# The last layer of a two-block model carries 512 token columns instead of 528

## The chip, the cores and the metric

The kernel runs on one NeuronCore of a Trainium2 chip. The core has a matrix engine (TensorE, in the profile PE, with the loading of its weights as PEld), a vector engine (VectorE, DVE), a scalar engine (ScalarE, ACT), GpSimd (POOL) and SyncE (SP), which issues most DMA transfers. Each engine works off its own list of instructions in order; semaphores join the lists. The metric is the device time of one execution, in microseconds (us), as the median of the runs.

## The reference

Two blocks of two layers each, in float32, on 512 tokens of 1024 features. The first block isn't touched here. The second puts 16 learned meta tokens ahead of the 512 real ones (528 in all) and runs `hybrid_layer` twice; only the real tokens are returned:

```python
h = jnp.concatenate([meta, x], axis=1)              # 16 + 512 tokens
for i in range(DEPTH):                              # DEPTH = 2
    h = hybrid_layer(h, ...)
return rmsnorm_2(h, final_norm)[:, N_META:]

def hybrid_layer(h, ...):
    proj = rmsnorm_2(h, attn_norm_g) @ w_in          # fq fk fv flog rq rk rv rg
    fox = fox_attention(fq, fk, fv, logf)            # 8 heads of 64, causal, with forget gates
    ret = retention_chunkwise(rotate(rq), rotate(rk), rv)      # 4 heads of 128
    mix = concat(fox, silu(rg) * head_groupnorm(ret))
    h = h + mix @ w_out
    hn = rmsnorm_2(h, ffn_norm_g)
    return h + (silu(hn @ w_gate) * (hn @ w_up)) @ w_down      # 2816 hidden features
```

Attention and retention are causal, so the real tokens need the meta tokens' keys and values. Of the second layer nothing else of the meta tokens reaches the output.

## The kernel before, in words

Activations lie feature-major: 128 features on the partitions, the 528 tokens as columns, eight such tiles for 1024 features. Every large product is done in `gemm` (lines 188 to 197). A float32 operand is split into a high part of 11 mantissa bits and a rest; three products (lines 195, 196, 197) stand for one. So an output tile of 128 features takes 8 k-tiles x 3 products per group of columns. A product writes at most 512 columns (one PSUM bank), and `groups` (line 199) cuts 528 into two groups of 264: a tile is 48 products of 264 columns. In block 1, which has 512 tokens, a tile is 24 products of 512.

`wunit` (line 163) brings 512 KB of weights: a DMA issued by SP, the high part on ACT (line 170), the rest on DVE (line 171); three buffers for each.

`layer2` (line 1720) does in this order, for each of the two layers:
- it writes the eight tiles of the residual to DRAM (`xs`), makes the forget gates, and the attention's values by token (`values2`, lines 1532 to 1534, products of 512 columns, and 1529 and 1530 for the meta tokens);
- four pairs of attention heads (loop at 1752): the query tile and the key tile of the pair (`proj2`, DVE at 1765 applies the norm), then `fox_pair`: first the meta tokens' own queries (`fox_meta`, lines 1550 to 1577), then four blocks of 128 queries, each with scores (1593, 1599), mask, maximum, exponential, division, transposes (1618, 1628) and the weighted values (1633, 1637);
- `values2` for the retention, then four heads (loop at 1780): query and key tile with rotation (`rotated`, DVE at 1651 to 1654), then `retention` (scores 1667 and 1674, values 1683 to 1688, group norm with transposes at 1710);
- four gate tiles (loop at 1790), the output projection (8 tiles) added to the reloaded residual, a norm (`lead`, `lead_end`, `spread`), 22 pairs of gate and up tiles (`up`, 1826), and the down projection in six pieces (1852; k of 2, 4, 4, 4, 4, 4 tiles), added to the residual by DVE at 211.

PSUM has eight banks: four slots S of one bank and two slots D of two banks. In the attention and in the heads of the retention the large products have two S slots and the small ones the other two; elsewhere the large products have all four. A tile of 264 columns takes a whole slot as well.

A scheduling layer sets the order on each engine. It takes instructions by priority, and within a layer by their place in the code, as their inputs come ready by its own estimates, and so puts the next pair's or head's large products between the small ones of the attention. What it has set is fixed in the program.

Of the kernel before, what the change touches and what calls it, by code (L numbers as in the profile page):

```python
# [113 lines left out]
class Kern:  # L114
# [10 lines left out]
    # ------------------------------------------------------------------ tiles  # L125
# [19 lines left out]
    def band(self, b):  # L145
        """Instructions inside take the scheduling priority b (less is sooner)."""
# [7 lines left out]
    def many(self, ring, cnt, rows, n, dt=F32):  # L154
        """cnt aps [rows, n] and their tiles; short ones share a tile by twos."""
# [6 lines left out]
    # ---------------------------------------------------------------- weights  # L162
# [20 lines left out]
    def split(self, src, hi, lo):  # L183
        """hi: 11 mantissa bits of src, lo: the other 12."""
# [3 lines left out]
    def gemm(self, o, ts, w, k_w, x):  # L188
        """o += w[:, k_w[i]].T @ x[i][:, ts] over i, in three passes."""
# [14 lines left out]
    def acc_tile(self, pg, wu, ks, h, x, n, ga):  # L204
        """x += ga * (w @ h)"""
# [20 lines left out]
    def sq_add(self, ring, accs, x, i, n, cnt=KT):  # L226
        """Sum of squares of cnt tiles in two tiles: all but the last, the last."""
# [51 lines left out]
    def norm_split(self, ring, rb, out, xs, n, A, sh, ks=range(KT)):  # L279
        """h = x * rstd * A (+ sh), as hi / lo parts."""  # L280
# [15 lines left out]
    # ----------------------------------- norm whose scale is applied afterwards  # L296
    def lead(self, ring, k, x, g, hl, acc, first=None):
        """Residual tile k [128, 528] is final: x * g as hi / lo parts, sum of squares.

        first = (gain, its square, sum of squares before the gain): x is scaled by the gain in place first.  # L300
        """
        nc = self.nc
        xl = x[:, NM:L2]
# [22 lines left out]
        elif k == KT - 1:  # L326
            sq = ring.new([P, L2])
            nc.scalar.activation(sq, x, AF.Square)
            self.rest = (sq[:, NM:L2], self.ones[:, 0:1], sq[:, 0:NM], sq)
        else:  # L330
            sq = ring.new([P, L2])
# [12 lines left out]
    def lead_end(self, ring, pr, acc, acc1=None):  # L344
        """1/rms by token rows: columns 0-3 for the real tokens, column 4 for the meta tokens."""
# [1374 lines left out]
    def layer2(self, l):  # L1720
# [8 lines left out]
        for k in range(KT):  # L1729
            nc.sync.dma_start(out=xs[k], in_=X[k])  # L1730
# [368 lines left out]
```

## Time and profile before

| what | us |
|---|---|
| median of three runs (3163.07 to 3173.02) | 3165.82 |
| profiled execution: its span (no other time of it is given) | 3163.6 |
| PE busy in the span | 3064.9 |
| DVE busy | 1892.6 |
| ACT busy | 1182.7 |
| last layer from its first attention pair to the end | 2480.7 to 3163.6 |
| of this, the MLP behind the output projection, to the end of its last product | 2757.1 to 3147.2 |

A matmul's duration in the profile runs from its entry to the modelled end of its pipeline, so successive ones overlap; 264 columns take 285 ns, but the next begins 122 ns later. What a stream of them costs is read from how many begin in a stretch, or from the start of one to the start of the next. Start times are us from the span's start.

### The profile page before, as it was taken

The page shows a single profiled execution, that of the slowest core. Times are in us where ns is not written, and L with a number is a line of the kernel's source. Part 1 is how long each engine was busy: PE and PEld are TensorE (multiplying, and loading weights), DVE is VectorE, ACT ScalarE, POOL GpSimd, SP SyncE. Part 2 cuts the span into 40 slices and gives each one's busy share as a digit, 9 for nine tenths or more (in the row PEclk, how much of TensorE's full clock was granted, in tenths as well). Part 3 has the DMA queues.
Part 4 walks back from the last instruction along what each step waited for, and adds up shares of the span by engine and source line. Part 5 has one row for each costly group of instructions (what it writes and reads, how often), then busy time and mean ns, then how long its engine had stood idle before and what let it go on. Part 6 is the DMA issues. An engine that isn't in the chain of part 4 may idle for free.

```text
span 3163.6 us, 48896 instructions
## 1 busy us (share of the span) xinstructions
PE 3064.9 (97%) x19434; PEld 2687.5 (85%) x19434; DVE 1892.6 (60%) x3935; ACT 1182.7 (37%) x2119; POOL 105.4 (3%) x287
## 2 busy tenths in 40 slices
PE   8899899999999998999999999999999999999998
PEld 4778879788888877778888888999999888999998
DVE  5877756787655766444436656555555556555554
ACT  4545554253333455433334431322223331322222
POOL 1000000000000000000000000000001000000000
PEclk9999999999999999999999999999999999999999
DMA  8554526755555432122333212232323212322222
GB/s 302 171 193 144 159 91 191 234 164 171 172 166 170 131 118 60 61 80 93 94 99 110 66 54 71 95 91 90 92 89 110 65 54 71 95 90 92 92 89 67
DMA packets 138147, 367.55 MB, mean 116 GB/s; under 512 B 14864, under 2 KB 42960, under 8 KB 137920
## 3 DMA queue, kind: packets, MB, share of 16 engines
q1 hardware_dynamic: 135760, 361.72, 36.2%
q8 instruction: 153, 2.51, 0.3%
q10 hardware_dynamic: 1728, 2.24, 0.2%
q14 instruction: 74, 0.61, 0.1%
q0 software_dynamic: 432, 0.48, 0.1%
HBM read 349.16 MB, written 15.12 MB: 115 GB/s over the span
## 4 chain that ended last, share of the span: by engine, by line
PE 83%; DVE 6%; DMA 6%; ACT 3%; issue 1%; POOL 1%; SPq 0%; ACTq 0%; DVEq 0%; POOLq 0%
PE S L195 21%; PE S L196 21%; PE S L197 21%; DVE wl L171 2%; PE S L1006 1%; DMA wr<-wmod 1%; PE D L978 1%; ACT wh L170 1%; PE S L1637 1%; PE D L1593 1%; PE S L994 1%; PE S L1532 1%; DVE wr L428 1%; PE S L1534 1%; PE D L1688 1%
## 5 line engine op out<-in xcount | busy, mean ns | idle before, releaser
L195 PE MATMUL S<-A,wh 128*128 128x264 f32 (+2 forms) x5104 | 1619.3, 318 | 14.6 <-ACT A L290 3.8
L197 PE MATMUL S<-A,wl 128*128 128x264 f32 (+2 forms) x5104 | 1613.5, 316 | 7.1 <-DVE wl L171 7.0
L196 PE MATMUL S<-A,wh 128*128 128x264 f32 (+2 forms) x5104 | 1611.6, 316 | 3.8 <-DVE A L291 2.4
L195 PEld LDWEIGHTS S<-A,wh 128*128 128x128 f32 x5104 | 965.1, 189 | 87.2 <-issue 8.0
L197 PEld LDWEIGHTS S<-A,wl 128*128 128x128 f32 x5104 | 964.8, 189 | 71.4 <-DVE wl L171 11.1
L196 PEld LDWEIGHTS S<-A,wh 128*128 128x128 f32 x5104 | 964.5, 189 | 70.0 <-DVE A L291 5.7
L170 ACT CAST wh<-wr 128x1024 fp32r<-128x1024 f32 (+1 forms) x474 | 495.1, 1045 | 1393.1 <-PE S L196 838.6
L171 DVE TENSOR_TENSOR wl<-wr,wh 128x1024 fp32r<-128x1024 f32 (+1 forms) x474 | 576.3, 1216 | 346.5 <-ACT wh L170 336.0
L428 DVE SCALAR_TENSOR_TENSOR wr<-wr,B 128x512 f32<-128x512 f32 x224 | 149.2, 685 | 84.1 <-DMA wr<-wmod 84.0
L213 DVE SCALAR_TENSOR_TENSOR A<-S,mod,A 128x512 f32<-128x512 f32 x144 | 107.7, 749 | 114.4 <-PE S L197 114.1
L211 DVE TENSOR_TENSOR A<-A,S 128x264 f32<-128x264 f32 x224 | 93.7, 426 | 116.5 <-PE S L197 116.3
L186 DVE TENSOR_TENSOR A<-A,A 128x512 fp32r<-128x512 f32 (+3 forms) x168 | 102.3, 618 | 32.8 <-ACT A L185 32.5
L1834 DVE TENSOR_TENSOR A<-S,A 128x264 f32<-128x264 f32 x88 | 38.0, 432 | 121.1 <-PE S L197 115.5
L185 ACT CAST A<-A 128x512 fp32r<-128x512 f32 (+3 forms) x168 | 93.1, 562 | 24.8 <-DVE A L1799 18.1
L1842 DVE SCALAR_TENSOR_TENSOR A<-A,S 128x264 f32<-128x264 f32 x88 | 37.8, 429 | 80.4 <-PE S L197 75.8
L1006 PEld LDWEIGHTS S<-B,B 128*128 128x128 f32 x416 | 53.6, 195 | 17.1 <-issue 5.5
L1006 PE MATMUL S<-B,B 128*128 128x96 f32 x416 | 55.7, 277 | 4.7 <-ACT A L1011 2.3
L223 POOL TENSOR_TENSOR rnr<-rnv,mhalf 128x4 f32<-128x4 f32 (+1 forms) x19 | 23.2, 1223 | 969.3 <-DVE rnv L222 581.5
L978 PE MATMUL D<-A,A 96*128 96x256 f32 (+1 forms) x144 | 54.6, 483 | 0.5 <-ACT A L948 0.5
L562 DVE SCALAR_TENSOR_TENSOR A<-A,cw,A 128x512 f32<-128x512 f32 (+1 forms) x84 | 52.8, 638 | 2.4 <-ACT A L559 0.8
L1061 ACT ACTIVATE A<-A 128x512 f32<-128x512 f32 x80 | 50.6, 632 | 2.2
L230 ACT ACTIVATE A<-A 128x512 f32<-128x512 f32 (+1 forms) x66 | 33.6, 535 | 46.9 <-DVE A L213 35.1
(402 smaller groups left out, 2903.2 us busy)
## 6 DMA issues: line engine op xcount, KB each, us to landing
wr<-wmod SPq DMA_DIRECT2D x112, 512.0 KB, 4.1
wr<-wup SPq DMA_DIRECT2D x96, 512.0 KB, 3.6
wr<-wdn SPq DMA_DIRECT2D x96, 512.0 KB, 3.8
wr<-win SPq DMA_DIRECT2D x78, 512.0 KB, 4.0
wr<-wg SPq DMA_DIRECT2D x44, 512.0 KB, 3.5
wr<-wu SPq DMA_DIRECT2D x44, 512.0 KB, 3.6
wr<-wd SPq DMA_DIRECT2D x44, 512.0 KB, 3.5
wr<-wout SPq DMA_DIRECT2D x40, 512.0 KB, 3.7
```

Source lines behind the costliest of these rows:

```text
L170: nc.scalar.copy(hi, raw)
L171: nc.vector.tensor_sub(lo, raw, hi.bitcast(F32))
L185: self.nc.scalar.copy(hi, src)
L186: self.nc.vector.tensor_sub(lo, src, hi.bitcast(F32))
L195: nc.tensor.matmul(o, wh[:, k_w[i]], xh[:, ts], start=(i == 0), stop=False)
L196: nc.tensor.matmul(o, wh[:, k_w[i]], xl[:, ts], start=False, stop=False)
L197: nc.tensor.matmul(o, wl[:, k_w[i]], xh[:, ts], start=False, stop=(i == nk - 1))
L211: nc.vector.tensor_add(x[:, ts], x[:, ts], ps)
L213: nc.vector.scalar_tensor_tensor(out=x[:, ts], in0=ps, scalar=ga, in1=x[:, ts], op0=ALU.mult, op1=ALU.add)
L428: nc.vector.scalar_tensor_tensor(out=wf if i == len(which) - 1 else self.junk, in0=wf, scalar=1.0, in1=self.cb[s * 2 + hf], op0=ALU.mult, ...
L978: nc.tensor.matmul(sc[:, off : off + nk], qT[h][:, ts], kT[h], start=True, stop=True)
L1006: nc.tensor.matmul(yp, pT[:, kt], V[j][:, h * MD : h * MD + MD], start=(kt == 0), stop=(kt == tot // P - 1))
```

## The change

In the last layer the queries, the gates, the retention's outputs and all behind them (out projection, norm, MLP, final norm) are made for the 512 real tokens alone, in one group of 512 columns. Keys, values, forget gates and the rotation's tables keep 528. `fox_meta` and the retention's meta outputs go, as do the meta column of the two norms behind. Layer 0 is as it was.

```diff
 def layer2(self, l):
+    final = l == DEPTH - 1
+    n = N if final else L2
+    o0 = L2 - n
+    every = self.groups(L2)
+    kept = [slice(o0, L2)] if final else every
-    xs = self.tl(self.dr, [KT, P, L2], F32, f"xt{l}")
+    xs = self.tl(self.dr, [KT, P, n], F32, f"xt{l}")
...
-            for o, ts in self.proj2(pg, l, which * 4 + p2, h):
+            for o, ts in self.proj2(pg, l, which * 4 + p2, h, every if which else kept):
...
-        self.fox_pair(pm, p2, two[0], two[1], v, vblk, mix[p2])
+        self.fox_pair(pm, p2, two[0], two[1], v, vblk, mix[p2], not final)
...
-        q = self.rotated(qr, pg, l, 8 + hd, h, rope)
+        q = self.rotated(qr, pg, l, 8 + hd, h, rope, kept)
...
-        k = self.rotated(qr, pg, l, 12 + hd, h, rope)
-        o = A.new([P, L2])
-        before = self.retention(pm, l, hd, q, k, v, o)
+        k = self.rotated(qr, pg, l, 12 + hd, h, rope, every)
+        o = A.new([P, n])
+        before = self.retention(pm, l, hd, q, k, v, o, kept)
...
-        for o, ts in self.proj2(pg, l, 16 + hd, h):
+        for o, ts in self.proj2(pg, l, 16 + hd, h, kept):
...
-    X = [A.new([P, L2]) for _ in range(KT)]
+    X = [A.new([P, n]) for _ in range(KT)]
...
-        for ts in self.groups(L2):
+        for ts in self.groups(n):
...
-                self.acc_tile(pg, w, kk, hs, X[m], L2, None)
+                self.acc_tile(pg, w, kk, hs, X[m], n, None)
 def proj2(self, pg, l, m, h, tss):
-    for ts in self.groups(L2):
+    for ts in tss:
 def fox_pair(self, pr, p2, q, k, v, vblk, o, meta):
-    self.fox_meta(pr, q, k, vb, o)
+    if meta:
+        self.fox_meta(pr, q, k, vb, o)
 def retention(self, pr, l, hd, q, k, v, out, tss):
-    for ts in self.groups(L2):
+    for ts in tss:                                   # scores with the meta keys
...
-    nc.tensor.matmul(om, pmt[:, 0:NM], v[4][:, hs], start=True, stop=True)
+    if meta:
+        nc.tensor.matmul(om, pmt[:, 0:NM], v[4][:, hs], start=True, stop=True)
...
-    for rows, cnt, src in ((NM, 1, om.unsqueeze(1)), (P, 4, ot)):
+    for rows, cnt, src in ([(NM, 1, om.unsqueeze(1))] if meta else []) + [(P, 4, ot)]:
 def lead_end(self, ring, pr, acc, acc1=None):
-    tok.append((4, NM, acc[:, 0:NM], sm_, one))
+    if meta:
+        tok.append((4, NM, acc[:, 0:NM], sm_, one))
 def spread(self, rb, r, meta):
+    if rb.shape[-1] == N:
+        for t in range(4):
+            o = dd[:, 0, t * P : t * P + P]
+            nc.tensor.matmul(o, r[:, t : t + 1].broadcast_to([P, P]), self.ident, start=True, stop=True)
+        nc.scalar.copy(rb, dd[:, 0])
+        return
```

The order on the engines moves where the attention and the retention of the last layer stand. Line numbers of the changed kernel are its own. On PE, in the first attention pair, third block of queries (S and D are PSUM slots, B the probabilities, wh and wl a weight unit's parts), before:

```order
L1618 MATMUL S_4229_23080<-ident_69,B_4228_23075 128x128 x3
L1599 MATMUL D_4247_23139<-A_4180_22894,A_4173_22830 128x264 x2
L197 MATMUL S_4268_23249<-A_4064_22243,wl_4267_23245 128x264
L195 MATMUL S_4268_23249<-A_4066_22245,wh_4266_23244 128x264
L196 MATMUL S_4268_23249<-A_4067_22246,wh_4266_23244 128x264
L197 MATMUL S_4268_23249<-A_4066_22245,wl_4267_23245 128x264
L1618 MATMUL S_4235_23098<-ident_69,B_4234_23093 128x128 x3
L1628 MATMUL S_4237_23104<-ident_69,metaP_4224_23067 32x128
L195 MATMUL S_4268_23249<-A_4068_22247,wh_4266_23244 128x264
L196 MATMUL S_4268_23249<-A_4069_22248,wh_4266_23244 128x264
L197 MATMUL S_4268_23249<-A_4068_22247,wl_4267_23245 128x264
L195 MATMUL S_4268_23249<-A_4070_22249,wh_4266_23244 128x264
```

and in the changed kernel, where transposes are line 1637, scores 1618 and weighted values 1652 and 1656:

```order
L1637 MATMUL S_4222_23033<-ident_69,B_4221_23028 128x128 x3
L1618 MATMUL D_4234_23072<-A_4178_22866,A_4172_22829 128x264
L1637 MATMUL S_4228_23051<-ident_69,B_4227_23046 128x128 x3
L1618 MATMUL D_4240_23092<-A_4179_22867,A_4173_22830 128x264
L1647 MATMUL S_4230_23057<-ident_69,metaP_4217_23020 32x128
L1618 MATMUL D_4240_23092<-A_4179_22867,A_4173_22830 128x264
L1652 MATMUL S_4232_23061<-mT_4231_23059,A_4155_22809 128x128
L1656 MATMUL S_4232_23061<-B_4223_23037,A_4150_22797 64x128
...
L1656 MATMUL S_4232_23061<-B_4229_23055,A_4150_22797 64x128
...
L195 MATMUL S_4254_23138<-A_4078_22257,wh_4252_23133 128x512
```

Before, large products of 264 columns stood between the transposes and the weighted values of this block; now none does until the block is done, and the ones that follow have 512 columns.

On DVE, in the fourth block of the same pair, before (1765 reads the next pair's query and key tiles out of PSUM, 264 columns at a time, between the softmax's steps):

```order
L1608 TENSOR_SCALAR mx_4242_23123<-mx_4242_23123 128x1
L1604 TENSOR_TENSOR D_4247_23139<-D_4247_23139,fmask_14888 128x128
L1765 TENSOR_TENSOR A_4257_23176<-S_4262_23212,A_4121_22566 64x264
L1607 TENSOR_REDUCE mx_4248_23143<-D_4247_23139 128x1
L1613 RECIPROCAL smx_4243_23124<-smx_4243_23124 128x1
L171 TENSOR_TENSOR wl_4351_23591<-wr_4349_23589,wh_4350_23590 128x1024
L1614 TENSOR_SCALAR B_4244_23127<-B_4244_23127,smx_4243_23124 128x528
L186 TENSOR_TENSOR A_4157_22814<-S_4239_23108,A_4156_22813 128x128
L1608 TENSOR_SCALAR mx_4248_23143<-mx_4248_23143 128x1
L1622 COPY B_4246_23137<-S_4245_23132 128x512
```

and in the changed kernel, where 1793 is that line:

```order
L1627 TENSOR_SCALAR mx_4241_23096<-mx_4241_23096 128x1
L186 TENSOR_TENSOR A_4157_22814<-S_4232_23061,A_4156_22813 128x128
L1633 TENSOR_SCALAR B_4237_23080<-B_4237_23080,smx_4236_23077 128x528
L1793 TENSOR_TENSOR A_4249_23128<-S_4254_23138,A_4121_22566 64x512
L1632 RECIPROCAL smx_4242_23097<-smx_4242_23097 128x1
L1641 COPY B_4239_23090<-S_4238_23085 128x512
L1633 TENSOR_SCALAR B_4243_23100<-B_4243_23100,smx_4242_23097 128x528
L1793 TENSOR_TENSOR A_4250_23129<-S_4254_23138,A_4121_22566 64x512
L171 TENSOR_TENSOR wl_4336_23470<-wr_4334_23468,wh_4335_23469 128x1024
```

The next pair's query tile is now read out in two instructions of 512 columns, both behind the maxima of the fourth block; before, its halves and the key tile's first half were read from the second block on.

On PE, in the retention's first head, before (1667 are the scores with the meta keys, 1674 the others, 1683 the meta output, 1686 and 1688 the values):

```order
L1667 MATMUL S_4546_24503<-A_4529_24367,A_4536_24433 16x264
L1667 MATMUL S_4547_24506<-A_4529_24367,A_4536_24433 16x264
L195 MATMUL S_4562_24549<-A_4064_22243,wh_4560_24544 128x264
...
L196 MATMUL S_4562_24549<-A_4069_22248,wh_4560_24544 128x264
L1674 MATMUL S_4548_24509<-A_4529_24367,A_4536_24433 128x512
L1674 MATMUL S_4550_24513<-A_4529_24367,A_4536_24433 128x384
L1683 MATMUL D_4556_24525<-A_4528_24363,B_4545_24502 16x128
L1686 MATMUL D_4556_24525<-A_4528_24363,B_4545_24502 128x128
L197 MATMUL S_4562_24549<-A_4068_22247,wl_4561_24545 128x264
...
L197 MATMUL S_4562_24549<-A_4070_22249,wl_4561_24545 128x264
L1674 MATMUL S_4552_24517<-A_4529_24367,A_4536_24433 128x256
L1688 MATMUL D_4556_24525<-A_4524_24355,B_4549_24511 128x128
```

and in the changed kernel, where these are 1688, 1695, 1708 and 1710:

```order
L1688 MATMUL S_4517_24286<-A_4501_24179,A_4507_24216 16x512
L1695 MATMUL S_4518_24289<-A_4501_24179,A_4507_24216 128x512
L195 MATMUL S_4532_24328<-A_4064_22243,wh_4530_24323 128x512
L196 MATMUL S_4532_24328<-A_4065_22244,wh_4530_24323 128x512
L1708 MATMUL D_4526_24305<-A_4500_24175,B_4516_24285 128x128
L1695 MATMUL S_4520_24293<-A_4501_24179,A_4507_24216 128x384
L1695 MATMUL S_4522_24297<-A_4501_24179,A_4507_24216 128x256
L1710 MATMUL D_4526_24305<-A_4496_24167,B_4519_24291 128x128
L1708 MATMUL D_4526_24305<-A_4500_24175,B_4516_24285 128x128
L1710 MATMUL D_4526_24305<-A_4496_24167,B_4519_24291 128x128
L197 MATMUL S_4532_24328<-A_4064_22243,wl_4531_24324 128x512
```

The scores follow each other more closely, with two large products between them where eight stood, and the meta output is gone.

## Rows read from the trace of the kernel before

**Rows 1.** The page, parts 1 and 4: engines over the span, and the chain that ended last.
```profile
span 3163.6 us, 48896 instructions
PE 3064.9 (97%) x19434; PEld 2687.5 (85%) x19434; DVE 1892.6 (60%) x3935; ACT 1182.7 (37%) x2119; POOL 105.4 (3%) x287
...
PE 83%; DVE 6%; DMA 6%; ACT 3%; issue 1%; POOL 1%; SPq 0%; ACTq 0%; DVEq 0%; POOLq 0%
```

**Rows 2.** Table by stretch: PE, weight load, DVE, ACT, POOL busy us (instructions), granted clock, DMA.
```profile
core 0: us, PE busy (x) PEld busy (x) DVE busy (x) ACT busy (x) POOL busy (x), PEclk, DMA share, GB/s
1500.00:1710.00 210.00, 210.00 (x909) 170.15 (x908) 91.76 (x104) 79.73 (x107) 0.00 (x0) 1.00 0.31 94
2480.67:2560.87 80.20, 80.00 (x587) 67.38 (x586) 55.48 (x195) 32.84 (x101) 6.85 (x28) 1.00 0.13 41
2560.87:2583.52 22.65, 22.58 (x135) 16.21 (x134) 15.57 (x57) 9.36 (x31) 1.51 (x8) 1.00 0.15 48
2613.17:2634.16 20.99, 20.99 (x144) 17.68 (x143) 14.93 (x41) 3.07 (x5) 1.54 (x2) 1.00 0.18 51
2780.00:3100.00 320.00, 320.00 (x2631) 320.00 (x2630) 166.72 (x264) 76.41 (x91) 0.00 (x0) 1.00 0.29 91
3147.30:3163.60 16.30, 4.31 (x28) 3.87 (x28) 5.75 (x13) 2.02 (x4) 1.52 (x2) 0.65 0.34 129
```

**Rows 3.** Groups by line and shape, PE, 1500 to 1710: count, busy us, mean ns.
```profile
L195 PE MATMUL S<-A,wh 128*128 128x512 f32 x303 | 119.1, 394 | 0.0
```

**Rows 4.** The same for 2780 to 3100.
```profile
L195 PE MATMUL S<-A,wh 128*128 128x264 f32 x877 | 249.2, 284 | 0.0
```

**Rows 5.** Who waited for whom, PE, 2475 to 3164: us in total, times, longest.
```profile
PE D L384 <- DVE rcol L373: 1.9, 2, 1.5
PE S L358 <- ACT A L328: 1.1, 1, 1.1
PE S L1710 <- DVE B L1705: 0.6, 1, 0.6
```

**Rows 6.** PE in order of time, first attention pair: start us, duration us, line, shapes.
```profile
2480.67 0.27 PE L1555 MATMUL S<-A,A 65*16 65x16 f32 x4
2480.87 0.76 PE L1593 MATMUL D<-A,A 65*128 65x144 f32 x4
...
2485.29 0.19 PE L1570 MATMUL S<-ident,ms 16*32 16x16 f32 x1
2485.41 0.39 PE L195 MATMUL S<-A,wh 128*128 128x264 f32 x1
...
2485.97 0.39 PE L1575 MATMUL S<-mTs,A 32*128 32x16 f32 x2
2486.29 0.39 PE L195 MATMUL S<-A,wh 128*128 128x264 f32 x1
```

**Rows 7.** The page, part 5: DVE reading a finished tile of 512 and of 264 columns.
```profile
L213 DVE SCALAR_TENSOR_TENSOR A<-S,mod,A 128x512 f32<-128x512 f32 x144 | 107.7, 749 | 114.4 <-PE S L197 114.1
L211 DVE TENSOR_TENSOR A<-A,S 128x264 f32<-128x264 f32 x224 | 93.7, 426 | 116.5 <-PE S L197 116.3
```

**Rows 8.** PE in order of time, first head of the retention.
```profile
2616.83 0.39 PE L1683 MATMUL D<-A,B 16*16 16x128 f32 x2
2617.15 0.48 PE L1686 MATMUL D<-A,B 16*128 16x128 f32 x2
```

**Rows 9.** The chain in order of time, behind the last product: start us, us, what.
```profile
3147.19 0.44 DVE A L211
...
3148.73 0.22 PE S L357 x2
...
3151.80 2.42 PE D L384 x10
...
3154.24 0.49 ACT A L386
3154.74 0.18 ACT A L387
```

More of the change, by code (lines that the diff above doesn't have):

```diff
@@ L302, in lead @@
         nc = self.nc
-        xl = x[:, NM:L2]
+        n = x.shape[-1]
+        o = n - N
+        xl = x[:, o:n]
         if first is not None:
@@ L326, in lead @@
         elif k == KT - 1:
-            sq = ring.new([P, L2])
+            sq = ring.new([P, n])
             nc.scalar.activation(sq, x, AF.Square)
-            self.rest = (sq[:, NM:L2], self.ones[:, 0:1], sq[:, 0:NM], sq)
+            self.rest = (sq[:, o:n], self.ones[:, 0:1], sq[:, 0:NM] if o else None, sq)
         else:
-            sq = ring.new([P, L2])
+            sq = ring.new([P, n])
             nc.scalar.activation(sq, x, AF.Square)
@@ L350, in lead_end @@
         ts = [slice(t * P, t * P + P) for t in range(4)]
-        tok = [(t, P, acc[:, NM:L2][:, ts[t]], sq[:, ts[t]], g) for t in range(4)]
-        tok.append((4, NM, acc[:, 0:NM], sm_, one))
+        meta = sm_ is not None
+        accl = acc[:, NM:L2] if meta else acc
+        tok = [(t, P, accl[:, ts[t]], sq[:, ts[t]], g) for t in range(4)]
+        if meta:
+            tok.append((4, NM, acc[:, 0:NM], sm_, one))
         if acc1 is not None:
@@ L1577, in fox_meta, with fox_pair @@
         pr.drop(ps)
-    def fox_pair(self, pr, p2, q, k, v, vblk, o):
+    def fox_pair(self, pr, p2, q, k, v, vblk, o, meta):
         nc = self.nc
@@ L1649, in rotated @@
         t = ring.new([P, L2])
-        for o, ts in self.proj2(pg, l, m, h):
+        for o, ts in self.proj2(pg, l, m, h, tss):
             nc.vector.tensor_mul(q[:, ts], o, rope[0][:, ts])
@@ L1656, in rotated, with retention @@
         return q
-    def retention(self, pr, l, hd, q, k, v, out):
+    def retention(self, pr, l, hd, q, k, v, out, tss):
         nc = self.nc
@@ L1663, in retention @@
         nc.sync.dma_start(out=dt_, in_=self.a["decay"][hd])
+        meta = tss[0].start == 0
         pmt = B.new([NM, L2])
-        for ts in self.groups(L2):
+        for ts in tss:
             ps = pr.new([NM, ts.stop - ts.start])
@@ L1711, in retention @@
             B.drop(gt)
-            dst = out[:, 0:NM] if cnt == 1 else out[:, NM:L2]
+            dst = out[:, 0:NM] if cnt == 1 else out[:, NM:L2] if meta else out
             nc.scalar.activation(
@@ L1792, in layer2 @@
                 next(before)
-            t = qr.new([P, L2])
-            th = qr.new([P, L2])
-            for o, ts in self.proj2(pg, l, 16 + hd, h):
-                nc.vector.tensor_mul(t[:, ts], o, rb[:, ts])
+            t = qr.new([P, n])
+            th = qr.new([P, n])
+            for o, ts in self.proj2(pg, l, 16 + hd, h, kept):
+                nc.vector.tensor_mul(t[:, ts.start - o0 : ts.stop - o0], o, rb[:, ts])
             nc.scalar.activation(th, t, AF.Tanh, scale=0.5)
@@ L1820, in layer2 @@
         r, _ = self.lead_end(lr, pg, acc)
-        rb = lr.new([P, L2])
+        rb = lr.new([P, n])
         self.spread(rb, r, True)
@@ L1838, in up @@
             nc.vector.tensor_mul(t, t, rb)
-            for ts in self.groups(L2):
+            for ts in self.groups(n):
                 p1 = pg.new([P, ts.stop - ts.start])
@@ L1845, in up @@
                 pg.drop(p1)
-            (p,), tiles = self.hl(tr, 1, L2)
+            (p,), tiles = self.hl(tr, 1, n)
             self.split(t, *p)
@@ L1860, in layer2 @@
                 lr.drop(rb)
-                acc = lr.new([P, L2])
-                final = l == DEPTH - 1
+                acc = lr.new([P, n])
                 if not final:
-                    h, ht = self.hl(hr, 8, L2)
+                    h, ht = self.hl(hr, 8, n)
             per = 8 // nk
@@ L1882, in layer2 @@
         r, _ = self.lead_end(lr, pg, acc)
-        rb = lr.new([P, L2])
+        rb = lr.new([P, n])
         self.spread(rb, r, True)
```

32 lines of the change are left out of this document (18 added, 14 removed).

## The prediction

> **What bounds the kernel now.** I read the page first. PE is busy for 97% of the span, and the chain that ended last lies on PE for 83% of it [rows 1]. That share alone proves little, since a matmul's duration covers its pipeline; so next come the table by stretch and the waits, for the last layer only. From 2780 to 3100, inside the MLP, PE is busy for 320 of 320 us, DVE for 166.7 and ACT for 76.4, at a granted clock of 1.00, the higher of the two levels [rows 2]. The waits that the trace puts down to PE from 2475 to the end come to 3.6 us, most of them in the tail [rows 5]. So this layer lasts as long as PE's list of instructions does, and what the change is worth is what it takes off that list.
>
> **The large products.** From 2780 to 3100, 2631 products of 264 columns begin (three lines of 877) [rows 2, 4]: one in 320/2631 = 121.6 ns. From 1500 to 1710, in block 1's MLP, 909 products of 512 columns begin (three lines of 303) [rows 2, 3]: one in 210/909 = 231.0 ns. Two of 264 cost 243.2 ns, one of 512 costs 231.0: 12.2 ns less a pair. By proportion, 16 columns of 528 less would be 7.4 ns; the rest comes with half as many instructions. The pairs that become one: 12 tiles (4 queries of the attention, 4 of the retention, 4 gates) x 24 = 288; output projection 8 x 24 = 192; gate and up 22 x 2 x 24 = 1056; down projection 8 x 22 x 3 = 528; together 2064. Saved: 2064 x 12.2 ns = 25.2 us. The price of 512 is from another layer, but from the same lines with the same operands, four PSUM slots and DVE at 44% of the stretch [rows 2], so I take it as it is. As bounds, a large product could cost what a weight load and its neighbours make it here, at worst the same 243 ns as the two (no gain).
>
> The Trainium skill (TensorE: Matmul & The Clock Gate, Back-to-back issue gap) gives for isolated matmuls at full clock the columns over 2.4 GHz plus 2.5 ns: 112.5 ns and 215.8 ns as estimates from that page, a gain of 9.2 ns a pair and 19.0 us in all. The rows lie above both figures, by 9 and by 15 ns, so I go by the rows; the page's result is a rival below.
>
> **What hides the other engines.** DVE now reads a whole tile at once: near 749 ns for 512 columns where it took 2 x 426 [rows 7], so it does less, not more. A tile lasts PE 24 x 231 = 5.5 us, and in the MLP four slots hold four tiles, so an eviction that is 0.3 us longer is hidden. Weight units last PE 5.5 us instead of 5.8; their DMA takes 0.29 of the engines' time, their casts part of the DVE and ACT times above [rows 2]; nothing there comes near its limit. The residual goes out and back at 512 columns instead of 528, beside products.
>
> **The attention.** Three things change. First, `fox_meta` goes. From the start of each of its entries to the next one: 0.20 us (1555), 0.12 (1570), 0.32 (1575) [rows 6]; with about 0.2 us for the change from large to small products and back around the last, 0.84 us a pair. Secondly, the order is coarser. The first three pairs take 80.20/3 = 26.73 us each, with 96 products of 264 (11.68 us), which leaves 15.05 for the attention. The fourth, from its start to the first large product behind its last values, is unlike them: its large products are those of `values2` at 512 columns, 35 of them by the program's order (8.09 us), and it takes 22.65, which leaves 14.56 [rows 2]. So the coarser mixture costs 0.5 us less. In the changed kernel the first three pairs look like that fourth one: between the pair's first scores and its last weighted values stand 24 products of 512 and 21 of 264, 8.1 us, where 87 of 264 (10.6 us) stood. A pair then is 14.56 - 0.84 + 24 x 0.231 + 48 x 0.1216 = 25.1 us, 1.6 less than 26.73, of which 0.3 is already in the large products. Beyond these: 3 x 1.3 + 0.84 = 4.7 us. Thirdly, less cover. The new wait is that of the transposes of the third block for their softmax, with no large product ahead of them; behind it on PE stand the rest of the pair and the next key tile, on DVE the reading of the next query tile. The fourth pair has had just this thin cover and shows no wait worth a row [rows 5], with DVE busy 15.6 of 22.65 us [rows 2], so I put 0.5 us on the whole. The bounds are 0 and 9 us, the latter if the chain of softmaxes already sets the pace (worked out below).
>
> **The retention.** A head takes 20.99 us [rows 2]. The meta output's product goes (0.32 us to the next entry [rows 8]), and its transpose with it (nearest row: 0.12 for 1570 [rows 6]); the score with the meta keys is one product instead of two, and large and small products change places four times less a head, near 0.1 us each. That is 0.9 us a head; 3.6 for four, bounds 1.5 and 5. Two large products instead of eight now stand between the head's first scores and their use, and the key tile's second half has to be rotated in that time: three reads and an addition of 264 columns, near 4 x 0.43 = 1.7 us, beside scores of 528, 512 and 384 columns that last about as long. I put a wait of 0.25 us on each head: 1.0 in all.
>
> **Norms and tail.** The norm behind the output projection loses two products with a column of ones and a transpose, near 0.4 us. Behind the last product everything stands on the path: the last addition covers 512 columns (0.75 instead of 0.44 us, +0.31); the sum of squares loses one of five pairs of products at 0.22 each (-0.4); one of five transposes in 2.42 us goes (-0.45); one copy of 512 columns stands where 0.49 + 0.18 stood (about -0.1) [rows 7, 9]. The clock falls there, to a mean of 0.65 [rows 2], and will again. Net: -0.6 us.
>
> **The sum.** -25.2 - 4.7 - 3.6 - 0.4 - 0.6 + 0.5 + 1.0 = -33.0 us. The profiled execution had a span of 3163.6 us, so 3130.6 after; the median of the runs stood 2.2 above that span, and I keep these 2.2: 3132.8 us.
>
> **Rivals.**
> - *The attention and the heads wait.* If the chain of softmaxes sets the pace, the stretch from a pair's first scores to its last values stays what it is, 26.73 less nine products behind it (1.1 us) and less 0.84, 24.8 us, and the 27 key products now behind it (3.3 us) come on top: 28.1 a pair, 3.0 more than above, 9.0 for three. With 0.5 more a head: 3132.8 + 9.0 + 2.0 - 0.5 = 3143. For it: DVE is busy for 55.5 of 80.2 us there [rows 2] and stands in the chain. Against it: the fourth pair's 22.65 us.
> - *The page's gap.* If a product of 512 saves 9.2 ns a pair, as the skill's formula has it, the large products give 19.0: 3139. Against it: both measured intervals.
> - *No gain on the products.* If a product of 512 here is as dear as two of 264, with no gain on 2064 pairs, what is left is 7.8 us: 3158, no change by measurement. Against it: 909 of them in rows.
> - *Slower: two slots.* In the attention and the heads the large products have two PSUM slots. A tile of 512 holds its slot for 5.5 us and until DVE has read it, and DVE reads it behind the softmax of the fourth block. If the second half of the keys finds that slot taken, PE stands, and with it everything behind. It would take over 4.1 us of standing in each of the four pairs and four heads (33/8) to be slower than before; with 5 us each: 3132.8 + 40 = 3173. Against it: in the order, 24 products of the first key half (2.9 us) and the small ones lie between, and the read comes ahead of them.
>
> **How the numbers follow.** My forecast 0.77, the waiting attention 0.11, the page's gap 0.05, no gain on the large products 0.04, two slots 0.03. Around the forecast: 1 us on the interval of a product, 2 on the retention, 2 on the attention's waits, 3 for the run: 3126 to 3140. Eight times in ten needs some of the waiting attention as well: 3125 to 3145. About 0.3% (9.5 us) is what a measurement can tell from no change. Faster by more: 0.77 + 0.11 + 0.05 = 0.93; the same 0.04; slower 0.03.
>
> **What would show it.** In the MLP of the changed kernel: 433 products begin in 100 us (231 ns each), PE without waits. Pairs of the attention from one start to the next: 25.1 us; 28 would be the first rival. Heads: 20.99 - 0.29 - 0.65 = about 20.0 us. From the end of the last product to the end of the span: 15.7 us instead of 16.3. I am wrong if the interval of a product of 512 in the MLP is over 236 ns, or if PE shows waits of more than 1 us a pair.

## The result, and the profile after

The changed kernel took 3126.7 us (median of four runs, 3118.1 to 3132.4) against 3166.2 (four of before, 3163.1 to 3173.0): a ratio of 0.987, with a 95% interval of 0.985 to 0.989. The forecast was 3132.8, range 3125 to 3145, faster. The time lies in the range, 6 us below the point.

The page of the changed kernel, parts 1 and 4, answers to [rows 1]:

```profile
span 3119.1 us, 44395 instructions
PE 3023.0 (97%) x17310; PEld 2557.1 (82%) x17310; DVE 1868.5 (60%) x3755; ACT 1179.8 (38%) x2101; POOL 102.3 (3%) x281
...
PE 71%; issue 13%; DVE 6%; DMA 5%; ACT 3%; POOL 1%; POOLq 0%; DVEq 0%; ACTq 0%; SPq 0%
```

PE has lost 2124 instructions and 41.9 us of busy time; its share of the span is the same. The 13% of "issue" is no new wait. The chain in order of time (start us, us, what) has nearly all of it in one piece:

```profile
2737.58 368.78 issue
```

This is the MLP, through which PE is busy all the time, as the next table shows: time without a wait is "issue" here.

The table by stretch for the same places as [rows 2]: three attention pairs, the fourth pair, one head, the inside of the MLP, the tail. Columns as there.

```profile
2470.30:2546.80 76.50, 75.46 (x495) 58.97 (x493) 54.31 (x168) 31.93 (x91) 6.85 (x28) 1.00 0.13 42
2546.80:2569.00 22.20, 22.16 (x131) 15.78 (x130) 14.98 (x51) 9.37 (x29) 1.57 (x8) 1.00 0.17 49
2597.86:2617.67 19.81, 19.81 (x115) 15.80 (x115) 13.54 (x32) 2.76 (x4) 1.01 (x1) 1.00 0.22 69
2800.00:3060.00 260.00, 260.00 (x1126) 211.06 (x1125) 129.78 (x156) 65.70 (x78) 0.00 (x0) 1.00 0.29 95
3102.50:3119.10 16.60, 4.36 (x25) 3.89 (x23) 5.93 (x11) 1.94 (x3) 1.01 (x1) 0.58 0.34 126
```

In the MLP 1126 products begin in 260 us, 433 in 100 us or 230.9 ns each: the number that the forecast named. The group behind it, and DVE's read of a finished tile, answer to [rows 4, 7]:

```profile
L195 PE MATMUL S<-A,wh 128*128 128x512 f32 x376 | 147.8, 393 | 0.0
...
L211 DVE TENSOR_TENSOR A<-A,S 128x512 f32<-128x512 f32 x32 | 22.0, 688 | 41.7 <-PE S L197 41.5
```

PE's waits from 2430 us to the end (in total, times, longest) answer to [rows 5]:

```profile
PE D L393 <- DVE rcol L380: 2.0, 2, 1.5
PE S L364 <- ACT A L331: 1.3, 1, 1.3
PE D L1612 <- ACT B L1630: 1.0, 1, 1.0
PE D L399 <- DVE rcol L380: 0.4, 1, 0.4
```

The third row is new: a score of the first pair waits 1.02 us for an exponential. The forecast called itself wrong at waits of more than 1 us a pair; the first pair is just at that limit, and the other three have no wait in this list. The wait of the retention's transposes [rows 5] is gone.

The layer, cut where PE's rows in order of time show the first product of a stage. The last product is the last of the MLP's large products. The forecast's terms are spread over the stages as its text places them; they add up to its −33.0.

| stage | before | after | change | forecast |
|---|---|---|---|---|
| gates, values, to the first pair's scores | 45.62 | 44.99 | −0.6 | −0.3 |
| three pairs | 80.19 | 76.50 | −3.7 | −4.3 |
| fourth pair, to the first head's scores | 52.11 | 51.06 | −1.1 | −1.1 |
| three heads | 63.07 | 59.45 | −3.6 | −2.8 |
| fourth head, gate tiles, output projection | 80.69 | 75.07 | −5.6 | −4.2 |
| norm, MLP, to the start of the last product | 389.94 | 369.73 | −20.2 | −19.7 |
| from there to the end | 16.73 | 16.99 | +0.3 | −0.6 |
| the layer from its first gate product | 728.35 | 693.79 | −34.6 | −33.0 |

The spans differ by 44.5 us. The other 9.9 lie ahead of the layer: it begins at 2435.25 before and at 2425.31 after, though every engine has the same instructions in the same order up to there.

### The profile page after: what moved, and what is told of

Read it like the earlier page. It is cut to its first block, busy times and chain, and to the rows that moved or that the text cites. A ratio compares the mean times of both kernels' runs of the same rounds, so it can differ in the third digit from the quotient of the medians.

```text
span 3119.1 us, 44395 instructions
## 1 busy us (share of the span) xinstructions
PE 3023.0 (97%) x17310; PEld 2557.1 (82%) x17310; DVE 1868.5 (60%) x3755; ACT 1179.8 (38%) x2101; POOL 102.3 (3%) x281
## 4 chain that ended last, share of the span: by engine, by line
PE 71%; issue 13%; DVE 6%; DMA 5%; ACT 3%; POOL 1%; POOLq 0%; DVEq 0%; ACTq 0%; SPq 0%
PE S L195 17%; PE S L196 17%; PE S L197 17%; DVE wl L171 2%; DMA wr<-wmod 1%; PE S L1021 1%; PE D L993 1%; DMA A<-nm 1%; ACT wh L170 1%; PE S L1656 1%; PE D L1612 1%; PE S L1547 1%; PE D L1710 1%; PE S L1549 1%; PE S L1548 1%
## 5 line engine op out<-in xcount | busy, mean ns | idle before, releaser
L195 PE MATMUL S<-A,wh 128*128 128x512 f32 (+2 forms) x4416 | 1496.0, 339 | 13.9 <-DVE A L1053 3.8
L197 PE MATMUL S<-A,wl 128*128 128x512 f32 (+2 forms) x4416 | 1492.1, 338 | 6.2 <-DVE wl L171 6.0
L196 PE MATMUL S<-A,wh 128*128 128x512 f32 (+2 forms) x4416 | 1492.3, 338 | 3.9 <-DVE A L291 2.4
L195 PEld LDWEIGHTS S<-A,wh 128*128 128x128 f32 x4416 | 834.0, 189 | 113.9 <-issue 7.2
L196 PEld LDWEIGHTS S<-A,wh 128*128 128x128 f32 x4416 | 834.2, 189 | 100.2 <-DVE A L291 5.7
L197 PEld LDWEIGHTS S<-A,wl 128*128 128x128 f32 x4416 | 834.2, 189 | 99.0 <-DVE wl L171 10.3
L211 DVE TENSOR_TENSOR A<-A,S 128x264 f32<-128x264 f32 (+1 forms) x168 | 85.3, 514 | 122.5 <-PE S L197 122.1
L1862 DVE TENSOR_TENSOR A<-S,A 128x264 f32<-128x264 f32 (+1 forms) x66 | 34.3, 519 | 126.9 <-PE S L197 124.2
L1870 DVE SCALAR_TENSOR_TENSOR A<-A,S 128x264 f32<-128x264 f32 (+1 forms) x66 | 34.0, 516 | 86.6 <-PE S L197 84.2
L1021 PEld LDWEIGHTS S<-B,B 128*128 128x128 f32 x416 | 52.8, 193 | 16.7 <-issue 4.5
```

Source lines behind the costliest of these rows:

```text
L195: nc.tensor.matmul(o, wh[:, k_w[i]], xh[:, ts], start=(i == 0), stop=False)
L196: nc.tensor.matmul(o, wh[:, k_w[i]], xl[:, ts], start=False, stop=False)
L197: nc.tensor.matmul(o, wl[:, k_w[i]], xh[:, ts], start=False, stop=(i == nk - 1))
L211: nc.vector.tensor_add(x[:, ts], x[:, ts], ps)
L1021: nc.tensor.matmul(yp, pT[:, kt], V[j][:, h * MD : h * MD + MD], start=(kt == 0), stop=(kt == tot // P - 1))
```

## The experiments

All are compared by the layer and its stages. Each starts from the changed kernel except the two named as before.

**1. The changed kernel again.** No edit.

> The changed kernel, nothing edited, for the size of the gain. In the two profiles the layer (from the first product of its forget gates to the end of the span) lasts 728.35 us before and 693.79 after, 34.6 less, and another 10 us lie in the first 700 us of the program, which the change does not touch. Theory: the 34.6 are the change's and the 10 are chance, so the layer is again within 1 us of 693.8 while its start moves by several us from run to run, and the ratio comes nearer to 3131/3166 = 0.989 than to the first 0.987. Rival: the change also makes the first 700 us shorter (all of the 10 us): then the layer begins near 2425 again and the ratio is 0.986.

Measured: ratio 0.988 (0.986 to 0.990), layer 693.83, its start at 2428.27; every stage is within 0.1 us of the first profile. The layer repeats to about a tenth of a microsecond, while its start moved by 3 us. That the ratio would come nearer to 0.989 did not happen.

**2. 512 columns only behind the mix.**

```diff
-        kept = [slice(o0, L2)] if final else every
+        kept = every
-            self.fox_pair(pm, p2, two[0], two[1], v, vblk, mix[p2], not final)
+            self.fox_pair(pm, p2, two[0], two[1], v, vblk, mix[p2], True)
```

(and the heads' output, its gates and the mix at 528; the output projection takes the mix's last 512 columns)

> Only the part behind the mix of the heads is carried at 512 columns: output projection, its norm, MLP, final norm. The gates, the attention with its meta queries and the retention are computed at 528 as before. Theory: the parts add up, so the layer takes 728.35 less 20.1 for the MLP and less about 2.4 for output projection and norm, plus 0.15 for the tail: 706; the pairs of the attention come 26.7 us apart, the heads 21.0, and the MLP lasts 370. Rival: the stages are not independent (for example the products of the attention are dearer for the mixture, and only the whole change gives 34.6): the layer at 702 or less, or 710 or more.

Measured: layer 705.38. The three pairs take 80.14, the three heads 63.12, as before; the MLP 369.78, as after. The parts add up, with 706 expected: −23.0 behind the mix, which leaves −11.6 for the rest.

**3. The same 512 tokens in two groups of 256.**

```diff
-        if n <= 512:
+        if n <= (256 if self.cut else 512):      # cut: the last layer
-        kept = [slice(o0, L2)] if final else every
+        kept = [slice(o0 + s.start, o0 + s.stop) for s in self.groups(N)] if final else every
```

> All 512 kept tokens in the last layer, but its products in two groups of 256 columns instead of one of 512 (queries, gates, output projection, MLP): the columns fall as in the change, the number of products does not. Two products of 256 cost 2 x 118.4 ns by block 1's interval, one of 512 costs 231.0, two of 264 cost 243.2. Theory (each product has a fixed part of 5 to 6 ns beside its columns): 2064 pairs x 5.8 ns = 12.0 us above the change: the layer at 706, the MLP at 379 instead of 370. Rival (only columns count, and the rest is the mixture): the layer at 694, the MLP at 370. A third: halves are taken over with a finer mixture, and the retention and attention lose more, the layer above 710 with the MLP at 379.

Measured: layer 709.19, MLP 378.60. Of the MLP's 20.2 us, 11.3 come from fewer columns and 8.9 from half as many products (5.6 ns for each of 1584). The table for 260 us inside its MLP:

```profile
2810.00:3070.00 260.00, 260.00 (x2198) 260.00 (x2197) 135.40 (x215) 64.09 (x76) 0.00 (x0) 1.00 0.30 93
```

One product of 256 begins every 118.3 ns, and the weight loads fill the whole stretch, as they did before [rows 2]; with 512 columns they fill 211 of 260 us. What lies above the expectation is in the heads, at 21.2 us each instead of 19.8. PE's waits (in total, times, longest) show 0.8 us of it in each of three heads:

```profile
PE S L1734 <- DVE B L1729: 2.3, 3, 0.8
PE D L1614 <- ACT B L1632: 1.2, 1, 1.2
```

Line 1734 holds the transposes of the retention's group norm. So this is the wait that stood once in the kernel before [rows 5], now in three heads, and not the one that the forecast put into the heads, which was on the rotation of the key tile's second half. That one shows neither here nor in the change.

**4. The meta queries back.**

```diff
-        if meta:
-            self.fox_meta(pr, q, k, vb, o)
+        self.fox_meta(pr, q if meta else k, k, vb, o if meta else [scratch, scratch])
```

> The change with fox_meta run in the last layer's four pairs again, on key columns in place of the query columns, which are not computed, into scratch that nobody reads. Theory: the small products cost what their entries took, 0.84 us a pair, 3.4 in all, but the first exponential of the layer is then fox_meta's again, its table load of 1.28 us lies beside other work, and the wait of 1.0 us in the first pair goes: the layer at 693.8 + 3.4 - 1.0 = 696.2, the second to fourth pair 0.84 longer (25.9), the first no longer than they are. Rival: the small products were hidden in PE's stream and the gain came from the order alone: pairs at 25.1, the layer at 693.

Measured: layer 696.32, and no wait of the first pair. Its three pairs, PE first:

```profile
2472.50:2498.76 26.26, 26.18 (x175) 20.44 (x172) 18.61 (x64) 11.63 (x35) 2.88 (x10) 1.00 0.12 42
2498.76:2525.01 26.25, 26.16 (x175) 20.62 (x172) 18.22 (x64) 10.50 (x34) 2.64 (x10) 1.00 0.11 41
2525.01:2550.82 25.81, 25.81 (x174) 20.59 (x171) 18.42 (x64) 10.42 (x34) 1.57 (x8) 1.00 0.12 42
```

Against experiment 7, where the table load is also out of the way, these pairs are 1.2, 1.2 and 0.8 us longer and the layer 4.1. The small products were not hidden: with what `fox_meta` does on the other engines they cost 1.0 us a pair, a little more than the 0.84 of the forecast.

**5. The attention's queries and keys in one product of three.**

```diff
-            nc.tensor.matmul(o, wh[:, k_w[i]], xh[:, ts], start=(i == 0), stop=False)
+            nc.tensor.matmul(o, wh[:, k_w[i]], xh[:, ts], start=(i == 0), stop=one and i == nk - 1)
+            if one:          # proj2 in the last layer
+                continue
```

> The change with the queries and keys of the last layer's attention in one of the three products of each weight block (the two correction products are left out), so 24 large products a pair instead of 72: 8 of 512 and 16 of 264 columns, 7.6 us less of PE's list. It asks how far the softmax chain is from setting the pace (the first rival of the forecast). Theory (PE's list sets the pace, the chain has room): a pair falls from 25.08 by most of the 7.6, to 18 to 20 us; DVE's 18.1 us of work a pair is the floor. Rival (the chain of softmaxes sets the pace already and the large products only fill its gaps): a pair stays above 23.5 us and PE shows waits of more than 5 us a pair.

Measured: pairs of 27.76, 26.01 and 18.80 us. Neither theory: with 7.6 us less on its list, PE took longer in two pairs (26.34 and 25.08 in the change). The first pair in four stretches:

```profile
2469.84:2475.30 5.46, 3.48 (x22) 2.92 (x20) 4.17 (x12) 3.89 (x6) 0.00 (x0) 0.99 0.43 147
2475.30:2481.20 5.90, 5.89 (x22) 4.57 (x22) 3.60 (x13) 1.89 (x5) 0.40 (x2) 0.50 0.00 1
2481.20:2488.50 7.30, 7.30 (x19) 5.11 (x18) 4.20 (x13) 1.26 (x5) 1.38 (x2) 0.50 0.19 72
2488.50:2497.60 9.10, 7.80 (x48) 5.78 (x47) 6.67 (x17) 4.31 (x12) 1.46 (x4) 0.88 0.39 118
```

PE stands still for 2.0 us in the first (the wait of the third row in the result, grown), and the granted clock, 0.99 there, is 0.50 in the next two, 1.2 GHz. What that costs is seen in PE's order of time there:

```profile
2481.17 2.50 PE L195 MATMUL S<-A,wh 128*128 128x512 f32 x5
2483.47 2.87 PE L1614 MATMUL D<-A,A 65*128 65x400 f32 x4
```

Five products of 512 columns in 2.30 us, 460 ns each instead of 230.9.

**6. The attention's queries alone in two groups of 256.**

```diff
-        ... self.proj2(pg, l, which * 4 + p2, h, every if which else kept)
+        ... self.proj2(pg, l, which * 4 + p2, h, every if which or not final else [slice(16, 272), slice(272, 528)])
```

> The change with only the attention's query tiles in two groups of 256 columns, 48 products instead of 24 a pair. By the fixed part of 5.6 to 5.8 ns a product that the run in halves showed, 24 more cost 0.14 us. Theory of the forecast (a coarser order of large and small products is worth 0.5 us a pair): the finer order costs about 0.3 to 0.5 more, the second and third pair come to 25.5 to 25.7. Rival (grain is worth nothing, what the forecast put down to it was something else): 25.2 and no wait.

Measured: second and third pair 25.35 and 25.04 (25.08 each in the change); the layer without its tail is 0.7 us longer, 7 ns for each of 96 products. The rival holds: within the 0.3 us by which single pairs scatter, the grain of the order is worth nothing beyond the products themselves.

**7. An exponential ahead of time.**

```diff
         nc.scalar.activation(e, e, AF.Ln, bias=1.0)
+        nc.scalar.activation(self.sm([8, 1], "warm"), e[:, 0:1], AF.Exp, scale=-1.0)
```

> The change with one exponential of 8 x 1 elements right behind the logarithm of the forget gates, so that the table of the exponential is loaded 30 us before the first softmax needs it. Theory (the 1.28 us load in the first softmax is what PE waits 1.0 us for): the first pair falls from 26.34 to about 25.1, PE's wait for L1630 there goes, and the layer falls from 693.8 to 692.6; the load lies beside products of the values. Rival (the first pair is longer for another reason, such as less of the value products beside it): the first pair stays near 26.3 and another wait takes the place.

ACT in order of time (start, us): in the kernel before, in the change, and in this one.

```profile
2481.76 1.28 ACT L1565 ACT_TABLE_LOAD   x1
2483.06 0.23 ACT L1565 ACTIVATE ms<-ms 16x32 f32<-16x32 f32 x1
```

```profile
2472.46 1.28 ACT L1630 ACT_TABLE_LOAD   x1 [0.99 <-DVE mx L1627]
2473.76 0.38 ACT L1630 ACTIVATE B<-D,mx 128x144 f32<-128x144 f32 x1
```

```profile
2447.96 1.28 ACT L1517 ACT_TABLE_LOAD   x1
2449.26 0.20 ACT L1517 ACTIVATE warm<-A 8x1 f32<-8x1 f32 x1
```

Before, `fox_meta`'s small exponential drew the load in; without it the load stands in the first softmax, ahead of the scores that wait for it. Moved 32 us ahead of the softmax, it costs nothing: pairs of 25.08, 25.08 and 25.06, layer 692.22. Shown as expected.

**8. The kernel before against itself.** No edit.

> The kernel before, nothing edited, timed against itself, for the 5 us by which the whole program has been faster than its last layer accounts for. The runs so far: nine of before have a mean of 3166.0 us, nine of the change 3125.7, a difference of 40.3, of which the last layer accounts for 34.6. Theory (chance of the first 700 us): the last layer starts anywhere from 2424 to 2440 in before as well, the ratio is 1.000 within 0.002, and in this profile the layer is again 728.3. Rival (something in the changed program makes the first 700 us shorter): the profile of before has its stretch from 300 to 500 us again with some 20 products fewer than the change's 693 in 300 to 400 us, and its layer starts near 2435.

Measured: ratio 0.999 (0.998 to 1.000), layer 729.15, its start at 2435.65. Of products, 688 begin from 300 to 400 us, only 5 fewer than the change's 693 and not some 20 (the first profile of before has 672). The layer's difference holds with a second profile of before. As to the first 700 us, the start speaks for the rival and the products do not.

**9. The change, the early exponential, a short tail.**

```diff
-        for ts in self.groups(n):                     # acc_tile
+        for ts in cut or self.groups(n):              # the last output tile: 384 and 128 columns
-            nc.scalar.activation(sq, x, AF.Square)    # lead, last tile
+            for c in [slice(0, n)] if hl else [slice(0, 384), slice(384, N)]:
+                nc.scalar.activation(sq[:, c], x[:, c], AF.Square)
```

> The version that the runs point to: the change, the early exponential of the run before this one, and the last output tile of the MLP in 384 and 128 columns (its additions and its sums of squares too), so that behind the last product only 128 columns are added and squared instead of 512. Theory: first pair at 25.1; from the last large product to the end 17.0 less 0.17 (the product), less about 0.45 (the addition), less about 0.3 (the square): 16.1 at the same clock, and the layer at 693.8 - 1.3 - 0.9 = 691.6. Rival (the shorter idle time saves nothing, since the output's DMAs end at their own time): the tail at 16.8 to 17.0 and the layer at 692.5. The total then is about 2 us under the change's 3126, less than its runs differ among each other.

Measured: layer 691.37; from the start of the last product to the end 14.96 us, with 0.7 us more ahead of it since that product starts later. The tail first in the change, then here, DVE and ACT in order of time:

```profile
3102.54 0.69 DVE L211 TENSOR_TENSOR A<-A,S 128x512 f32<-128x512 f32 x1 [0.69 <-PE S L197]
3103.26 0.63 ACT L331 ACTIVATE A<-A 128x512 f32<-128x512 f32 x1 [1.39 <-DVE A L211]
...
3103.95 0.38 PE L364 MATMUL S<-ones,A 128*128 128x1 f32 x2 [1.33 <-ACT A L331]
```

```profile
3116.55 0.29 DVE L211 TENSOR_TENSOR A<-A,S 128x128 f32<-128x128 f32 x1 [0.73 <-PE S L197]
...
3116.87 0.31 ACT L332 ACTIVATE A<-A 128x128 f32<-128x128 f32 x1 [0.50 <-DVE A L211]
```

The addition and the square take 0.60 us together instead of 1.32. The layer is 2.4 us shorter than the change's, where 2.2 was expected; 0.85 of this lies between experiment 7 and here. The total, 3126.5 (ratio 0.988, 0.986 to 0.989), can't be told from it, since runs of one kernel differ by 13 us.

**10. The residual's DRAM tensor as large as before.**

```diff
-        xs = self.tl(self.dr, [KT, P, n], F32, f"xt{l}")
+        xs = self.tl(self.dr, [KT, P, L2], F32, f"xt{l}")
```

> The change with the residual put aside in a DRAM tensor of 8 x 128 x 528 as before (only 512 of each row written and read) instead of 8 x 128 x 512: the one thing of the change that lies in DRAM. Asks where the 5 to 7 us come from that the whole program has gained ahead of the last layer, with the same instructions in the same order there. Theory (what lies in DRAM behind that tensor has moved, and the first 700 us, whose waits are for weights, see it): the runs come back to a mean of 3126 + 6 = 3132, and the last layer starts near 2436. Rival (nothing to do with it): a mean of 3126, a start of 2424 to 2433, the layer at 693.8.

Measured: ratio 0.987 (0.985 to 0.989), mean of four runs 3124.4, start 2431.99, layer 693.61. The rival: the size of that tensor has nothing to do with it.

**11. The kernel before with the early exponential.** The edit of experiment 7.

> The kernel before with the early exponential alone: two more instructions of ScalarE in each of block 2's layers. Theory: before, the load of the exponential's table was hidden behind fox_meta's, so the layer stays at 728.4 to 729.2 and the total at a ratio of 1.000. Rival for the table: the load cost before as well, and the layer falls by 0.5 to 1. It also asks whether a program with other instructions in the last layer has another start of it by that alone: if so its start is not near 2435.5 as in the two profiles of before, and its mean differs from 3167 by several us.

Measured: ratio 1.000 (0.999 to 1.001), layer 728.48, mean of twelve runs 3166.7. The first pair is 0.3 us shorter (26.74 for 27.04), so the load was hidden before but for that, and this edit moves neither the total nor its mean.

**12. Experiments 5 and 7 together.** Both edits.

> The run with one product of three for the attention's queries and keys (the correction products are left out), with the early exponential beside it. In that run PE stood 2.0 us in the first pair for the exponential's table load, the granted clock was 0.99 before and 0.50 for the 13 us after, and the first two pairs took 27.76 and 26.01, longer than with all products; the third, at 0.92, took 18.80. Theory (the chain of softmaxes has room, and what made the first two pairs long is the clock after the idle time): with the load early the clock stays near 1.00, all three pairs take 18 to 20 us, the layer comes to 667 to 670. Rival (the chain sets the pace wherever large products are few; the third pair is short because values stand behind it): the first two pairs stay above 23 us with PE waits of more than 2 us each, the layer above 678.

Measured: pairs of 22.69, 27.36 and 18.87 us, layer 680.76. The first two pairs, each in stretches:

```profile
2465.89:2473.00 7.11, 6.32 (x38) 5.19 (x37) 6.71 (x22) 3.63 (x9) 0.40 (x2) 1.00 0.33 114
2473.00:2480.00 7.00, 7.00 (x42) 5.14 (x43) 6.71 (x18) 3.41 (x11) 1.39 (x2) 1.00 0.24 77
2480.00:2488.60 8.60, 7.01 (x30) 4.88 (x28) 5.15 (x15) 3.04 (x8) 1.46 (x4) 0.62 0.37 122
2488.60:2495.00 6.40, 5.61 (x24) 4.97 (x23) 5.50 (x18) 2.45 (x5) 0.40 (x2) 0.50 0.00 0
...
2508.00:2516.00 8.00, 8.00 (x35) 5.73 (x32) 4.15 (x10) 2.06 (x6) 1.06 (x2) 0.50 0.01 1
```

The clock stays at 1.00 through the first 14 us, as the theory had it, but neither side holds whole: the first two pairs and the layer come nearer to the rival. PE stands still again, for 1.08 us in the first pair and for 1.07 us in the second (start, us, and in brackets the idle time ahead):

```profile
2481.94 1.09 PE L1621 MATMUL D<-A,A 65*128 65x264 f32 x2 [1.08 <-ACT B L1633]
...
2505.04 0.41 PE L1640 MATMUL S<-ident,B 128*128 128x128 f32 x2 [1.07 <-DVE mx L1630]
```

Behind each the clock is at 0.50, as the stretches from 2488.60 and from 2508.00 show. An idle time of 1.34 us just ahead of the first pair and one of 0.69 us early in it, at 2464.8 and 2470.1, were followed by no fall (1.00 to 2480). So the attention is near the point at which its chain shows: take 30% of PE's list away and waits of about 1 us appear, and behind some of them the clock falls. What a pair would take with those waits at the full clock stays open; the best pair, the third of experiment 5, took 18.8 us at 0.92.

## Why the prediction was right

**The large products** carry the change, as forecast. 230.9 ns was measured for 231.0, and the MLP with its norm gave 20.2 us for 19.7. The interval of another layer's products carried over. The lines, the four slots and the spare time of DVE were alike; no run varied these one by one. Experiment 3 splits the 12.3 ns measured for a pair: 2 x (121.6 − 118.3) = 6.6 for 16 columns less, 2 x 118.3 − 230.9 = 5.7 for one product less. This answers the rival "no gain". It answers the rival of 19.0 us as well, since the second product costs 5.7 ns here. The Trainium skill (TensorE: Matmul & The Clock Gate, Back-to-back issue gap) charges an isolated product at full clock 2.5 ns beside its columns. The rows show over twice that, and they decide.

**The attention** was forecast at 25.1 us a pair and took 25.08, by a sum whose parts were not all right. `fox_meta` is worth 1.0 us a pair instead of 0.84 (experiment 4), and the "coarser mixture", put at 0.5, is worth nothing where it was tested alone (experiment 6). The two errors nearly cancel, so the agreement to 0.02 us is in part luck; what is left, 0.1 to 0.3 us a pair, is not assigned.

**The new waits** were placed wrongly. None came for the transposes of the third block, and none in the heads, where 1.0 us was put: a head lost 1.20 us, just the 0.9 and 0.29 of the sum without its 0.25. One came that the forecast had not seen: 1.02 us in the first pair, from a table load that had been cheap only because the work removed had triggered it (experiments 7 and 11). The forecast counted `fox_meta` as products that go; it did not ask what else its exponential did for the one behind it.

**The tail** seems to contradict the forecast (+0.3 for −0.6) if one profile is set against one. Three profiles with the tail of before (experiments 8 and 11 and the first) took 16.73, 17.15 and 17.52 us from the start of the last product, nine with that of the change 16.28 to 16.99: means of 17.13 and 16.63, −0.5, which is no more than the scatter within a group. Much of the scatter goes with the moment at which the clock falls, here before and then after (the clock stands ahead of the last two numbers):

```profile
3151.00:3152.00 1.00, 0.20 (x1) 0.20 (x2) 0.17 (x1) 0.00 (x0) 1.00 (x2) 1.00 0.00 0
3152.10:3153.00 0.90, 0.90 (x6) 0.90 (x5) 0.13 (x1) 0.00 (x0) 0.00 (x0) 0.50 0.00 0
```

```profile
3104.00:3105.00 1.00, 1.00 (x10) 1.00 (x10) 0.00 (x0) 0.65 (x1) 0.00 (x0) 1.00 0.00 0
3105.10:3106.00 0.90, 0.90 (x6) 0.90 (x5) 0.00 (x0) 0.00 (x0) 0.00 (x0) 0.50 0.00 0
```

In the first profile of before it falls 5.2 us behind the start of the last product, in the first of the change 2.9 us. At like moments the change is ahead by less than was forecast: 16.3 us for 16.7 where it falls after 5.2 to 5.4 us, 17.0 for 17.15 where it falls after 2.8 to 2.9 us. So the forecast's −0.6 was too much, for some −0.1 to −0.4 measured; which of the removed products, transposes and copies gave it was not tested one by one.

**The waiting attention** (the rival at 3143) was ruled out by the pairs and has its limit in experiments 5 and 12: there is room, but in the first two pairs not for another 7.6 us with the clock that these runs had. The third pair lost 6.3 of the 7.6. The two slots (3173) show no wait at all.

**The 6 us** that the time is below the forecast are mostly not the layer's: it gave 34.6 for 33.0. Nine runs of the change had a mean of 3125.7 and nine of before 3166.0, 40.3 apart. The rest, 5.7 us, lies ahead of the layer, where the forecast expected nothing. With it the time came to 1.7 us above the lower end of the range, and two of the first four runs lie below that end: that the total fell inside was in part luck. Eleven profiles with the change's layer in some form start it between 2423.7 and 2439.8 us (mean 2429.2), three with the layer of before between 2435.3 and 2440.4 (mean 2437.1), so the groups overlap, but the means of many runs do not. It is not the DRAM tensor (experiment 10), and one more exponential in each layer did not move it (experiment 11). On the whole the start goes with the granted clock ahead of it: its mean from the span's start to the layer is 0.987 in the two earliest (2423.7 and 2425.3), 0.982 and 0.980 in the two latest (2439.8 and 2440.4). Which of the two causes the other was not tested, and the mean clocks of the two groups of nine runs, 0.985 in both, don't account for 5.7 us. The cause of the 5.7 us stays open.

## What to carry to other kernels

Where one engine's list sets the time, price a new shape by the interval of the same instruction at that shape elsewhere in the same trace; here the sum of the parts then held, as the run with half of the change showed. Before removing work, look at what it triggers early for others (here a table load), since that cost doesn't go away with it. And compare by stages with fixed landmarks: up to the start of its last product the layer repeated to 0.1 us, where the total moved by 13.

## What was not expected of the hardware

- An idle time of 2.0 us in a PE stream thinned by 30% was followed by a granted clock of 0.50 for 13 us, and the first pair took longer with less work (27.76 us for 26.34; 22.69 in experiment 12, where its first 14 us ran at 1.00). The change's own wait of 1.0 us, in a denser stream, was followed by no fall (1.00 over the three pairs).
- A product of 128 columns costs nearly as much as one of 256. In experiment 9 they follow each other like this, some 0.11 us apart at a clock of 1.00, where 256 columns took 118.3 ns in experiment 3. The measured 256, 264 and 512 columns (118.3, 121.6, 230.9 ns) lie within 0.2 ns on one line of 0.44 ns a column and 5.7 ns a product; 128 columns would be 62 ns by it. The weight loads of these products begin 0.11 us apart as well (at 3115.62, 3115.73 and 3115.84), each taking 0.19 us. So loads can follow each other faster than the 118.3 ns at which they filled the stretch of experiment 3; that they set the pace only at 128 columns is a reading, not tested:

```profile
3115.79 0.28 PE L196 MATMUL S<-A,wh 128*128 128x128 f32 x1
3115.90 0.27 PE L197 MATMUL S<-A,wl 128*128 128x128 f32 x1
3116.01 0.28 PE L195 MATMUL S<-A,wh 128*128 128x128 f32 x1
3116.12 0.28 PE L196 MATMUL S<-A,wh 128*128 128x128 f32 x1
```

- The logarithm of the forget gates and the exponential behind it each load their table, 1.28 us a time. The Trainium skill (ScalarE: Activation LUTs, Table sets: the hidden batching unit) names a set that holds both and counts one load for a logarithm followed by an exponential. The rows of this program show two. In experiment 7 they follow each other, the logarithm's load (line 1516) first:

```profile
2444.83 1.28 ACT L1516 ACT_TABLE_LOAD   x1
2446.13 0.64 ACT L1516 ACTIVATE A<-A 8x528 f32<-8x528 f32 x1
...
2447.96 1.28 ACT L1517 ACT_TABLE_LOAD   x1
```
